# Eight wide and eight narrow products in a row, in place of wide and narrow in turn, in the first half of two MLPs

## The chip, the cores and the metric

The kernel runs on one core of a Trainium2 chip. The metric is the device time of one execution in microseconds. A core has five engines with queues of their own: TensorE (PE in the profile, with its weight loads listed apart as PEld), VectorE (DVE), ScalarE (ACT), GpSimd (POOL) and SyncE (SP), which here issues the DMA transfers.

## The reference, cut to what matters

A trunk of two layers on 256 tokens of width 1024. Layer 0 mixes tokens with differential attention, layer 1 with a sparse attention that picks keys by an indexer; each is followed by an MLP with a squared ReLU. All is float32.

```python
def sq_relu_mlp(h, w1, w2):          # h: 256 x 1024, w1: 1024 x 4096, w2: 4096 x 1024
    u = jax.nn.relu(h @ w1)
    return (u * u) @ w2

for i in range(DEPTH):               # 2
    h = rms_norm(x, norm_mix[i])
    mix = diff_attention(h, ...) if i % 2 == 0 else dsa_attention(h, ...)
    x = x + mix
    x = x + sq_relu_mlp(rms_norm(x, norm_mlp[i]), mlp_w1[i], mlp_w2[i])
```

## The kernel before, in words

TensorE multiplies in a shortened float32 format. To keep the precision, each operand is split in two: a high part (the value rounded to that format) and a low part (what the rounding left). A product A x B is then made of three: high x high, high x low and low x high. The weights arrive by DMA in units of 128 x 2048 (`raw`); `unit` splits each into `whi` (a copy on ACT, L146) and `wlo` (a subtraction on DVE, L147), in two to four pieces. There are four buffers of `whi` and four of `wlo`. The activations are split likewise into the two halves of a tile `act`: `hi`, `lo`, and `both`, a view of the two side by side.

An MLP goes through FF = 4096 in eight blocks of 512 columns. `up(b)` computes block b of h @ w1 transposed: the weights are the stationary operand and the 256 tokens the moving one. A block has four groups m of 128 columns, a group has eight steps k of 128 rows. In each step the high weights meet `both` in one wide product of 512 columns (L479; the left half of the PSUM tile `ps` collects high x high, the right half high x low), and the low weights meet `hi` in one narrow product of 256 columns, added into the right half (L480). `post` then adds the two halves, squares, and splits the result (L485 to L489). The second half of the MLP uses `mm3` (L151, L153, L155): three products of 512 columns each, with the activations stationary. The order is up(0), then for each b: up(b+1), second half of block b. In up(0) the steps are cut in two (k = 0 to 3 for all four groups, then 4 to 7), since the second half of h is finished late; two of its four tiles are `acc`, all others `wk` (four buffers each).

Outside the MLPs, generators (`spawn`, `tick`) lay the attention's small work between the products of `mm3`; `tick` is called in `mm3` alone. The instructions of an engine run in the order in which the framework laid them at compile time; it goes by the written order, but can put an instruction ahead of another where it reckons that operands are late, as it does with the transposes of `make_h` (L228) at the start of an MLP.

Of the kernel before, what the change touches and what calls it, by code (L numbers as in the profile page):

```python
# [45 lines left out]
def trunk(ctx: ExitStack, tc: tile.TileContext, x_in, pos_in, pack_in, wf, out):  # L46
# [11 lines left out]
    mm = nc.tensor.matmul  # L58

    def acc():  # L60
        return psum.tile([128, 512], F32, name="acc", bufs=4)

    def wk():
        return psum.tile([128, 512], F32, name="wk", bufs=4)
# [66 lines left out]
    def unit(cols=2048, dmas=1, pieces=1, between=None):  # L131
        raw = wraw.tile([128, 2048], F32, name="raw")
        hi = wsp.tile([128, 2048], F32R, name="whi")
        lo = wsp.tile([128, 2048], F32R, name="wlo")
        src = bass.AP(tensor=wf.tensor, offset=wf.offset + off[0], ap=[[cols, 128], [1, cols]])
        off[0] += 128 * cols
        step = cols // dmas
        for i in range(dmas):
            c = slice(i * step, (i + 1) * step)
            nc.sync.dma_start(raw[:, c], src[:, c])  # L140
            if between is not None and i == 0:
                between()
        step = cols // pieces
        for i in range(pieces):
            c = slice(i * step, (i + 1) * step)
            split[:] = [nc.scalar.activation(hi[:, c], raw[:, c], AF.Copy).ins]  # L146
            nc.vector.tensor_tensor(lo[:, c], raw[:, c], hi[:, c].bitcast(F32), op=OP.subtract)  # L147
        return hi[:, :cols], lo[:, :cols]

    def mm3(ps, ah, al, wh, wl, first, last):  # L150
        mm(ps, ah, wh, start=first, stop=False)  # L151
        tick()
        mm(ps, ah, wl, start=False, stop=False)  # L153
        tick()
        mm(ps, al, wh, start=False, stop=last)  # L155
        tick()
# [37 lines left out]
    def row_scale(need_s):  # L194

        ss = tiny.tile([128, 2], F32, name="rowss")
        for t in range(2):
            j = sc.tile([128, D], F32, name="qn")
            with tc.issue_after(behind[0]):
                nc.scalar.activation(j, x[t], AF.Square, accum_out=ss[:, t:t + 1])  # L200
        v = tiny.tile([128, 2], F32, name="rowv")
        nc.vector.tensor_scalar(v, ss, 1.0 / D, EPS, op0=OP.mult, op1=OP.add)
        s2 = tiny.tile([128, 2], F32, name="rows2")
        nc.vector.reciprocal(s2, v)
        s = None
        if need_s:
            s = const.tile([128, 2], F32, name=f"srow{need_s}")
            nc.vector.tensor_copy(s, rsqrt_start(v, [128, 2]))
        return s, s2

    def parts():

        a = act.tile([128, 2, 4, 256], F32R, name="act")
        return a[:, 0], a[:, 1], a

    def new_h():
        return [parts() for _ in range(2)]
# [244 lines left out]
    def mlp(h, after):  # L462
        NB = FF // 512
        us = {}
        y = None

        def up(b):
            u1 = [unit(pieces=4 if b < 2 else 2) for _ in range(2)]
            uh, ul, _ = parts()
            us[b] = (uh, ul)  # L470
            w = [tuple(a.rearrange("p (k n) -> p k n", n=256) for a in u) for u in u1]

            def group(ps, m, ks):

                wh, wl = w[m // 2]
                c = slice((m % 2) * 128, (m % 2) * 128 + 128)
                for k in ks:
                    hi, _, both = h[k // 4]
                    mm(ps.rearrange("p (a b) -> p a b", b=256), wh[:, k, c], both[:, :, k % 4], start=k == 0, stop=False)  # L479
                    mm(ps[:, 256:], wl[:, k, c], hi[:, k % 4], start=False, stop=k == 7)  # L480

            def post(ps, m):
                r = sc.tile([128, 256], F32, name="sq")
                q = sc.tile([128, 256], F32, name="on")
                nc.scalar.activation(r, ps[:, 256:], AF.Copy)  # L485
                nc.vector.tensor_tensor(r, ps[:, :256], r, op=OP.add)  # L486
                nc.vector.scalar_tensor_tensor(q, r, 0.0, r, op0=OP.max, op1=OP.mult)  # L487
                nc.scalar.activation(uh[:, m], q, AF.Copy)  # L488
                nc.vector.tensor_tensor(ul[:, m], q, uh[:, m].bitcast(F32), op=OP.subtract)  # L489

            if b == 0:
                pss = [(acc() if m < 2 else wk()) for m in range(4)]
                for kk in range(2):
                    for m in range(4):
                        group(pss[m], m, range(kk * 4, kk * 4 + 4))
                for m in range(4):
                    post(pss[m], m)
            else:
                for m in range(4):
                    ps = wk()  # L500
                    group(ps, m, range(8))
                    post(ps, m)

        up(0)
        _, s2 = row_scale(0)
        for b in range(NB):
            if b + 1 < NB:
                up(b + 1)
            if y is None:
                y = [[acc() for _ in range(2)] for _ in range(2)]  # L510
            u2 = [tuple(a.rearrange("p (k n) -> p k n", n=D) for a in unit(pieces=2)) for _ in range(2)]
            uh, ul = us.pop(b)
            last = b + 1 == NB
            order = ([(t, u, n) for t in range(2) for n in range(2) for u in range(2)] if last else
                     [(t, u, n) for u in range(2) for t in range(2) for n in range(2)])
            for t, u, n in order:
                wh, wl = u2[u]
                for i in range(2):
                    k = u * 2 + i
                    c = slice(n * 512, n * 512 + 512)  # L520
                    tc_ = slice(t * 128, t * 128 + 128)
                    mm3(y[t][n], uh[:, k, tc_], ul[:, k, tc_], wh[:, i, c], wl[:, i, c],
                        b == 0 and k == 0, last and k == 3)
                if last and u == 1:
                    for j in range(2):
                        c = slice(n * 512 + j * 256, n * 512 + j * 256 + 256)
                        nc.vector.scalar_tensor_tensor(x[t][:, c], y[t][n][:, j * 256:j * 256 + 256],  # L527
                                                       s2[:, t:t + 1], x[t][:, c], op0=OP.mult, op1=OP.add)
                        after(t, n, j)


    h = new_h()
# [107 lines left out]
    for j in range(4):  # L640
        ps = [acc() for _ in range(2)]
# [11 lines left out]
    h = new_h()  # L653
# [3 lines left out]
    h = h1  # L657
# [10 lines left out]
    cqh, cql, _ = parts()  # L668
# [102 lines left out]
    for n in range(2):  # L771
        ps = [acc() for _ in range(2)]
# [3 lines left out]
    for n in range(2):  # L776
        ps = [acc() for _ in range(2)]
        c = slice(n * 512, n * 512 + 512)
# [51 lines left out]
    h = new_h()  # L830
# [105 lines left out]
```

## Time and profile before

| | |
|---|---|
| median of 3 runs | 609.68 us (608.34 to 611.04) |
| the profiled execution | 610.02 us, span 607.4 us |
| instructions | 8479 |
| PE / DVE / ACT / POOL busy | 593.5 / 428.1 / 368.9 / 19.1 us |
| products at L479 and L480 | 512 each |

The span runs from the first to the last instruction; some 2.6 us of the execution's time lie around it. Busy times are added per engine and overlap between engines. The end of a matmul is modelled, and matmuls overlap on PE: their starts are what the timeline measures. In the timeline the first number is the start, the second the duration, both in us, and neighbours of the same kind are merged (x2), their duration running from the first start to the last end.

### The profile page before, as it was taken

The numbers are of one execution on the slowest core, as the hardware profiler recorded it, in microseconds if no ns is written. First come the engines' busy times: TensorE is split into PE (matmuls) and PEld (weight loads), VectorE is DVE, ScalarE is ACT, GpSimd is POOL, SyncE is SP. The second block draws the span as 40 slices with busy tenths as digits, with TensorE's granted clock in tenths as the row PEclk, the third lists the DMA queues.
The fourth block names the chain that finished last, engine by engine and source line by source line (L and its number), as shares of the span: only waits on it lengthen the run. The fifth ranks groups of instructions, "written<-read, shape, count | busy, mean of one in ns | idle before, by whom it ended". The sixth has DMA issues, their size and how long they took to land.

```text
span 607.4 us, 8479 instructions
## 1 busy us (share of the span) xinstructions
PE 593.5 (98%) x3072; PEld 488.2 (80%) x3072; DVE 428.1 (70%) x1067; ACT 368.9 (61%) x720; POOL 19.1 (3%) x53
## 2 busy tenths in 40 slices
PE   8989999999999999999999899999999999999997
PEld 6767678888888888888787686778888888888886
DVE  5799986579557557656598999766786565666552
ACT  6789987576445444445397589784854454455430
POOL 5600000000000000000000000000000000000000
PEclk9999999999999999999999899999999999999999
DMA  8753453335645564555453226424465555555301
GB/s 311 261 207 145 143 199 132 146 139 209 208 169 183 203 201 161 193 208 169 162 208 140 71 69 209 139 69 140 139 240 185 199 208 177 179 199 206 141 1 70
DMA packets 16025, 102.29 MB, mean 168 GB/s; under 512 B 1904, under 2 KB 2416, under 8 KB 4336
## 3 DMA queue, kind: packets, MB, share of 16 engines
q1 hardware_dynamic: 15696, 101.62, 47.4%
q8 instruction: 24, 0.39, 0.3%
q10 hardware_dynamic: 288, 0.13, 0.1%
q14 instruction: 17, 0.14, 0.1%
HBM read 100.70 MB, written 1.05 MB: 168 GB/s over the span
## 4 chain that ended last, share of the span: by engine, by line
PE 81%; DVE 10%; ACT 3%; POOL 3%; issue 3%; DVEq 0%; POOLq 0%; ACTq 0%
PE wk L479 18%; PE acc L153 15%; PE acc L155 15%; PE acc L151 15%; PE wk L480 9%; DVE wlo L147 4%; DVE s L411 2%; PE wk L429 2%; PE acc L479 1%; PE wk L400 1%; PE wk L228 1%; POOL ang L276 1%; PE wk L384 1%; POOL tp L275 1%; ACT whi L146 1%
## 5 line engine op out<-in xcount | busy, mean ns | idle before, releaser
L147 DVE TENSOR_TENSOR wlo<-raw,whi 128x1024 fp32r<-128x1024 f32 (+2 forms) x210 | 230.0, 1116 | 115.7 <-ACT whi L146 115.5
L146 ACT ACTIVATE whi<-raw 128x1024 fp32r<-128x1024 f32 (+2 forms) x210 | 197.9, 975 | 96.2 <-issue 46.1
L153 PE MATMUL acc<-wlo,act 128*128 128x512 f32 (+1 forms) x504 | 198.8, 394 | 0.6 <-DVE wlo L147 0.6
L151 PE MATMUL acc<-whi,act 128*128 128x512 f32 (+1 forms) x504 | 199.1, 395 | 0.1
L155 PE MATMUL acc<-whi,act 128*128 128x512 f32 (+1 forms) x504 | 198.5, 394 | 0.0
L479 PE MATMUL wk<-act,whi 128*128 128x512 f32 x480 | 169.8, 398 | 0.0
L480 PE MATMUL wk<-act,wlo 128*128 128x256 f32 x480 | 134.7, 281 | 0.0
L155 PEld LDWEIGHTS acc<-whi,act 128*128 128x128 f32 x504 | 95.3, 189 | 19.9 <-issue 1.7
L153 PEld LDWEIGHTS acc<-wlo,act 128*128 128x128 f32 x504 | 95.4, 189 | 19.7 <-DVE wlo L147 1.3
L151 PEld LDWEIGHTS acc<-whi,act 128*128 128x128 f32 x504 | 95.2, 189 | 19.5 <-issue 1.0
L479 PEld LDWEIGHTS wk<-act,whi 128*128 128x128 f32 x480 | 90.1, 188 | 22.0
L480 PEld LDWEIGHTS wk<-act,wlo 128*128 128x128 f32 x480 | 90.7, 189 | 0.5
L488 ACT ACTIVATE act<-on 128x256 fp32r<-128x256 f32 x64 | 26.3, 417 | 57.5 <-DVE on L487 57.5
L422 ACT ACTIVATE s<-s,nb,rs_r 128x128 f32<-128x128 f32 x64 | 34.2, 537 | 6.0 <-DVE nb L420 5.9
L489 DVE TENSOR_TENSOR act<-on,act 128x256 fp32r<-128x256 f32 x64 | 26.8, 424 | 14.5 <-ACT act L488 12.7
L485 ACT ACTIVATE sq<-wk 128x256 f32<-128x256 f32 x60 | 22.4, 375 | 17.6 <-PE wk L480 17.6
L487 DVE SCALAR_TENSOR_TENSOR on<-sq 128x256 f32<-128x256 f32 x64 | 26.6, 421 | 0.9
L486 DVE TENSOR_TENSOR sq<-wk,sq 128x256 f32<-128x256 f32 x60 | 24.9, 418 | 0.0
L232 ACT ACTIVATE act<-wk,pack 128x128 fp32r<-128x128 f32 x64 | 18.5, 377 | 8.1 <-PE wk L228 8.0
L234 DVE SCALAR_TENSOR_TENSOR act<-wk,pack,act 128x128 fp32r<-128x128 f32 x64 | 17.7, 344 | 3.6 <-ACT act L232 3.6
L429 PE MATMUL wk<-pack,s 128*128 128x128 f32 x72 | 15.7, 290 | 2.5 <-DVE s L594 1.7
L527 DVE SCALAR_TENSOR_TENSOR x<-acc,rows,x 128x256 f32<-128x256 f32 x16 | 7.0, 479 | 15.0 <-PE acc L155 15.0
(176 smaller groups left out, 435.6 us busy)
## 6 DMA issues: line engine op xcount, KB each, us to landing
raw<-in_w SPq DMA_DIRECT2D x91, 1024.0 KB, 4.8
x<-in_x SPq DMA_DIRECT2D x4, 256.0 KB, 4.5
raw<-in_w SPq DMA_DIRECT2D x4, 256.0 KB, 5.2
raw<-in_w SPq DMA_DIRECT2D x2, 512.0 KB, 5.8
raw<-in_w SPq DMA_DIRECT2D x1, 984.0 KB, 4.6
raw<-in_w SPq DMA_DIRECT2D x1, 840.0 KB, 4.8
out_dram<-x SPq DMA_DIRECT2D x3, 256.0 KB, 2.0
out_dram<-x SPq DMA_DIRECT2D x2, 128.0 KB, 1.7
```

The costliest lines, as they stand in the source:

```text
L146: split[:] = [nc.scalar.activation(hi[:, c], raw[:, c], AF.Copy).ins]
L147: nc.vector.tensor_tensor(lo[:, c], raw[:, c], hi[:, c].bitcast(F32), op=OP.subtract)
L151: mm(ps, ah, wh, start=first, stop=False)
L153: mm(ps, ah, wl, start=False, stop=False)
L155: mm(ps, al, wh, start=False, stop=last)
L422: nc.scalar.activation(p[:, TS[t]], s[:, TS[t]], AF.Exp, bias=nb[:, t:t + 1], scale=nsc[:, t:t + 1], accum_out=z[t])
L429: nc.tensor.transpose(pt[:, i * 128:(i + 1) * 128], p[:, i * 128:(i + 1) * 128], ident)
L479: mm(ps.rearrange("p (a b) -> p a b", b=256), wh[:, k, c], both[:, :, k % 4], start=k == 0, stop=False)
L480: mm(ps[:, 256:], wl[:, k, c], hi[:, k % 4], start=False, stop=k == 7)
L487: nc.vector.scalar_tensor_tensor(q, r, 0.0, r, op0=OP.max, op1=OP.mult)
L488: nc.scalar.activation(uh[:, m], q, AF.Copy)
L489: nc.vector.tensor_tensor(ul[:, m], q, uh[:, m].bitcast(F32), op=OP.subtract)
```

## The change

In `group`, the loop over the steps k is run twice. The first run issues the wide products of all steps, the second the narrow products. The operands, the PSUM tile and the flags of the first and last product stay as they are.

```diff
                 for k in ks:
-                    hi, _, both = h[k // 4]
-                    mm(ps.rearrange("p (a b) -> p a b", b=256), wh[:, k, c], both[:, :, k % 4], start=k == 0, stop=False)
-                    mm(ps[:, 256:], wl[:, k, c], hi[:, k % 4], start=False, stop=k == 7)
+                    mm(ps.rearrange("p (a b) -> p a b", b=256), wh[:, k, c], h[k // 4][2][:, :, k % 4],
+                       start=k == 0, stop=False)
+                for k in ks:
+                    mm(ps[:, 256:], wl[:, k, c], h[k // 4][0][:, k % 4], start=False, stop=k == 7)
```

## Rows read from the trace of the kernel before

**Rows 1.** The page: busy time of the engines, and the granted clock in 40 slices.
```profile
PE 593.5 (98%) x3072; PEld 488.2 (80%) x3072; DVE 428.1 (70%) x1067; ACT 368.9 (61%) x720; POOL 19.1 (3%) x53
...
PEclk9999999999999999999999899999999999999999
```
**Rows 2.** The page: the chain that ended last, shares by engine.
```profile
PE 81%; DVE 10%; ACT 3%; POOL 3%; issue 3%; DVEq 0%; POOLq 0%; ACTq 0%
```
**Rows 3.** The page's groups of instructions: busy us, mean ns, idle us before.
```profile
L479 PE MATMUL wk<-act,whi 128*128 128x512 f32 x480 | 169.8, 398 | 0.0
L480 PE MATMUL wk<-act,wlo 128*128 128x256 f32 x480 | 134.7, 281 | 0.0
...
L480 PEld LDWEIGHTS wk<-act,wlo 128*128 128x128 f32 x480 | 90.7, 189 | 0.5
```
**Rows 4.** Windows: an up block in each MLP (first, seventh of twelve later ones).
```profile
158.89:170.18 11.29, 11.29 (x65) 9.80 (x64) 7.78 (x13) 6.32 (x10) 0.00 (x0) 1.00 0.51 179
...
459.32:470.61 11.29, 11.29 (x65) 9.80 (x64) 7.78 (x13) 6.32 (x10) 0.00 (x0) 1.00 0.56 189
```
**Rows 5.** Waits of PEld: us in total, times, longest us.
```profile
PEld acc L479 <- DVE act L234: 0.2, 1, 0.2
```
**Rows 6.** Timeline of DVE ahead of the block at 158.89.
```profile
151.00 1.22 DVE L147 TENSOR_TENSOR wlo<-raw,whi 128x1024 fp32r<-128x1024 f32 x1
```
**Rows 7.** Timeline of PE in an up block: three pairs, narrow to narrow.
```profile
160.18 0.28 PE L480 MATMUL wk<-act,wlo 128*128 128x256 f32 x1
160.29 0.40 PE L479 MATMUL wk<-act,whi 128*128 128x512 f32 x1
160.52 0.28 PE L480 MATMUL wk<-act,wlo 128*128 128x256 f32 x1
160.64 0.40 PE L479 MATMUL wk<-act,whi 128*128 128x512 f32 x1
160.88 0.28 PE L480 MATMUL wk<-act,wlo 128*128 128x256 f32 x1
161.00 0.40 PE L479 MATMUL wk<-act,whi 128*128 128x512 f32 x1
161.24 0.28 PE L480 MATMUL wk<-act,wlo 128*128 128x256 f32 x1
```
**Rows 8.** Timeline of PE, start of the MLPs: two wide products eight pairs apart.
```profile
128.56 0.39 PE L479 MATMUL wk<-act,whi 128*128 128x512 f32 x1
...
131.33 0.39 PE L479 MATMUL acc<-act,whi 128*128 128x512 f32 x1
...
434.29 0.40 PE L479 MATMUL wk<-act,whi 128*128 128x512 f32 x1
...
437.12 0.40 PE L479 MATMUL wk<-act,whi 128*128 128x512 f32 x1
```
**Rows 9.** Timeline of PE, amid a second half: eight products apart.
```profile
150.05 0.39 PE L151 MATMUL acc<-whi,act 128*128 128x512 f32 x1
...
151.86 0.39 PE L155 MATMUL acc<-whi,act 128*128 128x512 f32 x1
```
**Rows 10.** Timeline of PE behind an up block's last narrow product.
```profile
170.06 0.28 PE L480 MATMUL wk<-act,wlo 128*128 128x256 f32 x1
170.18 0.40 PE L151 MATMUL acc<-whi,act 128*128 128x512 f32 x1
...
172.05 0.40 PE L155 MATMUL acc<-whi,act 128*128 128x512 f32 x1
```
**Rows 11.** Timeline of PE in block 0 of the first MLP.
```profile
127.28 0.40 PE L480 MATMUL acc<-act,wlo 128*128 128x256 f32 x2
...
127.75 0.28 PE L480 MATMUL acc<-act,wlo 128*128 128x256 f32 x1
```
**Rows 12.** Timeline of PE: products of 328 columns, eight apart.
```profile
311.30 0.31 PE L151 MATMUL acc<-whi,act 128*128 128x328 f32 x1
...
312.50 0.31 PE L155 MATMUL acc<-whi,act 128*128 128x328 f32 x1
```

## The prediction

> **What bounds the kernel now.** I read the page first. TensorE is busy for 593.5 of 607.4 us, no other engine for more than 428.1, and the clock it was granted is at the full level (2.4 GHz) but for one slice [rows 1]. A busy PE is not yet a PE that sets the time, so the chain that ended last comes next: 81% of the span lies on PE in it [rows 2]. The grouped instructions then give the suspects: the wide products at L479 (stationary high weights, 512 columns) and the narrow ones at L480 (stationary low weights, 256 columns), one weight load before each; the loads' recorded length is 188 to 189 ns [rows 3]. The "mean ns" of a matmul is of no use for a sum: it is 398 and 281, yet a pair takes far less, because matmuls overlap. What one costs is the distance from its start to the next start, and that is read from the timeline.
>
> The windows show the stage. A first half of an MLP (L479/L480 for one block of 512 columns of FF, 32 pairs) takes 11.29 us with PE busy throughout [rows 4] (the stretches are cut at the block's first wide product and at the first product of what follows; x65 is the block's 64 and the end of the one before), so 353 ns per pair and 2.82 us for a group of eight pairs. The list of waits has a single entry for these two lines, 0.2 us at the first wide load of an MLP [rows 5]. So the up blocks are purely TensorE's own pace, and whatever the order of products saves or costs there reaches the end of the kernel one for one; nothing on DVE, ACT or the queues has to be argued away.
>
> **The change part by part.** Nothing is added or removed: 512 wide and 512 narrow products, 1024 loads, the same operands and the same PSUM tile. Only their order within a group changes: eight wide, then eight narrow (in the MLP's block 0, four and four, since its k loop is cut in two). The waits move a little. The high weights of k = 4 are now needed four narrow products (some 0.5 us) earlier, the low weights later. The last low weights of the block that starts at 158.89 are being written at 151.00 and take 1.22 us, and they come after the high ones they are the remainder of [rows 6]; with more than 6 us of cover this costs nothing, and without the cover it would cost at most those 0.5 us per half unit. The high weights' buffer is released some 0.9 us earlier, which helps ACT, which is no bound here. The end of a group, and with it the square and the PSUM tile's release, stays where it is.
>
> What is left is the pace of three kinds of neighbours.
>
> *In turn, as now.* Three pairs in a row, from 160.18 to 161.24, take 1.06 us [rows 7]: 353 ns a pair. From wide to narrow it is 0.23, 0.24 and 0.24 (mean 237), from narrow to wide 0.11, 0.12 and 0.12 (mean 117). All twelve later blocks take 11.29 us, so they go at this pace [rows 4]. The two stretches of block 0 and 1 together (64 pairs in each MLP) differ: eight pairs take 2.77 us in the first MLP and 2.83 in the second [rows 8]. The same code can thus run at 346 or 353 ns a pair; which of the two it falls into is fixed at its start and then stays.
>
> *Wide after wide.* In the second half of the MLP, products of 512 columns follow each other: eight starts in 1.81 us, 226 ns each [rows 9]. But not right after narrow ones: from the first wide product behind the block's last narrow one, eight starts take 1.87 us, 234 ns each [rows 10]. The slow pace thus lasts through as many products as a group has. In the new order every run of eight wide products stands behind narrow ones, so 1.87 is the nearer row, and I take it; 1.81 is the other bound.
>
> *Narrow after narrow.* Hardly in the trace. In one place the compiled order puts two narrow products side by side: the two together are recorded at 0.40 us, one alone at 0.28, so the second starts 0.12 after the first [rows 11]. Products of 328 columns follow each other every 150 ns (eight in 1.20 us) [rows 12]; with 226 for 512 columns this lies on a straight line of 0.41 ns a column, and the line gives 120 at 256 columns. From narrow to wide it is 110 to 120 ns, mean 117 [rows 7]. Below, the bound is 110, the shortest distance between the starts of two such products that the rows show. Above, it is the load's full recorded length, 189 [rows 3], if loads cannot follow each other so closely for eight in a row. I take 117, the mean over the transition that the trace shows most often.
>
> The Trainium skill, page "TensorE: Matmul & The Clock Gate", section "LDWEIGHTS (loading the stationary operand)", puts a load at its column count over 1.2 GHz, 107 ns for 128 columns, and the section "Back-to-back issue gap" puts 256 moving columns at about 109. By these a load just fits behind a narrow product, a group would take an estimated 2.60 us in either order, and the change would be worth nothing. The trace's 226 and 150 ns are above that page's 216 and 139, so its level is not this kernel's.
>
> The sum for a group: 1.87 + 8 x 0.117 = 2.80 us, against 2.82 in the twelve later blocks (48 groups) and 2.83 in the second MLP's start (8 groups): about 0.018 less, 56 times, 1.0 us gained. In the first MLP's start (8 groups) 2.77 becomes 2.80: 0.25 us lost. Together 0.75 us less. The profiled execution took 610.02 us, 607.4 of them span, 0.3 above the median of 609.68; so 609.3 for a profiled run and 608.9 as the median. A kernel of this spread (608.34 to 611.04) tells a change from none at about 0.5%, 3.05 us.
>
> **The rivals.**
>
> *The wide runs settle (faster).* If eight narrow products in a row leave less behind than narrow and wide in turn, the wide run goes at 1.81 and the narrow at 0.12: 2.77 a group, the pace the first MLP's start already has. That is 0.05 us in 56 groups, 2.8 us: 606.9. With narrow products at the lower bound of 0.11 too, a group is 2.69: 0.13 x 56 + 0.08 x 8 = 7.9 us, 601.8. For it: the start of the first MLP holds 346 ns per pair for 21 us, so the extra 7 ns are not a fixed price. Against it: after that very row of narrow ones a wide run still goes slowly [rows 10].
>
> *The narrow runs expose their loads (slower).* A wide product gives the next load 226 ns of cover, a narrow one little more than its own 107 ns (256 columns at the line's 0.41); now eight in turn need one load each. At present each load under a narrow product is followed by one under a wide one, which can make up for a late load. If each narrow product pays the 7 ns that a pair pays now, it takes 0.127, the group 2.89, and the kernel 0.07 x 56 + 0.12 x 8 = 4.9 us more: 614.6. At 150, the shortest pace that the trace holds over a long run with a load each, it would be 0.033 x 8 x 64 = 17 us more than the sum above: 626. At 189 the price is 37 us: 646. The point from which it decides (0.5% slower) is 0.124 for narrow after narrow. Against it: the loads of the 328-column run keep to the column line, and the one narrow pair stands at 0.12.
>
> *The order isn't kept.* The pair of narrow products side by side stands in a place where the code alternates [rows 11]: the compiled order is not the written one everywhere. If wide and narrow are laid in turn again, the time stays at 609.7.
>
> **How the numbers follow.** The likeliest case, a small gain by the sum, gets 0.50; its own range is 606.7 to 610.5 (narrow at 0.113 to 0.12, and the spread of the medians). The wide runs settle: 0.27. At 2.77 a group that just misses 0.5% (2.8 of 3.05 us), and any narrow pace under 0.12 passes it, so 0.22 of the 0.27 counts as faster. The narrow runs pay: 0.18, of it 0.17 beyond 0.5%. Order not kept: 0.05. So faster by over 0.5% 0.22, slower 0.17, within it 0.61. The range reaches into both rivals, from 605.6 (half way through the faster one) to 612.6, and leaves out about 0.1 on each side.
>
> **What would show it.** In the timeline of an up block: runs of eight L479 and eight L480; eight wide starts in 1.87 us (1.81 if the faster rival holds); narrow starts 0.117 apart (0.127 and more for the slower one). In the windows: an up block of 11.22 us instead of 11.29; 11.1 or less for the faster rival, 11.5 or more for the slower. Second halves unchanged. No new wait of L479 on the high weights. The prediction is wrong if the granted clock changes in the MLPs, or if stages outside them move by more than 1 us because the instructions there are laid in another order.

## The result, and the profile after

The changed kernel takes 606.59 us in the median of 5 runs (605.23 to 607.85), the one before 609.68 (608.34 to 611.04): ratio 0.9947, 95% interval 0.9923 to 0.9972. In a second series of five rounds, the run `after_again` below, the ratio was 0.9963 (0.9952 to 0.9975). So the change gains 2 to 3 us, 0.3 to 0.5%. The forecast was 608.9 with a range from 605.6 to 612.6: the sign was right and the range held the time, but the gain is some three to four times the 0.75 us of the sum.

The page after shows the same picture as [rows 1, 2]: PE sets the time, with 2.9 us less of it. One thing differs beside that: the one slice in which the granted clock was below its full level is gone.

```profile
PE 590.6 (98%) x3072; PEld 487.5 (81%) x3072; DVE 430.3 (71%) x1067; ACT 367.1 (61%) x720; POOL 19.0 (3%) x53
...
PEclk9999999999999999999999999999999999999999
...
PE 79%; DVE 13%; POOL 3%; issue 3%; ACT 3%; DVEq 0%; POOLq 0%; ACTq 0%
```

The windows of the changed kernel, cut as in [rows 4] (an up block, the second half behind it, the last up block): a later up block takes 11.15 us (11.146 by the start times in the trace) in place of 11.29, and the second half behind it 10.90 or 10.91, where the trace of before has 10.94. A row of a window has the stretch, its length, the busy time of PE, PEld, DVE, ACT and POOL with their instructions, the granted clock (1.00 is the full level), the share of DMA and its GB/s. First the second half of before, then the changed kernel:

```profile
170.18:181.12 10.94, 10.94 (x50) 9.02 (x49) 6.13 (x8) 4.71 (x6) 0.00 (x0) 1.00 0.51 191
```

```profile
159.33:170.48 11.15, 11.15 (x66) 9.83 (x65) 8.19 (x13) 6.91 (x11) 0.00 (x0) 1.00 0.64 220
170.48:181.38 10.90, 10.90 (x50) 9.01 (x49) 5.91 (x7) 4.00 (x6) 0.00 (x0) 1.00 0.46 159
...
567.67:578.81 11.14, 11.14 (x65) 9.82 (x64) 8.19 (x13) 6.91 (x11) 0.00 (x0) 1.00 0.20 83
```

The timeline of that first block answers to [rows 7] and [rows 10] at once, since runs of one kind are merged into a row. L478 is now the wide product, L481 the narrow one.

```profile
159.33 1.98 PE L478 MATMUL wk<-act,whi 128*128 128x512 f32 x8
161.14 1.11 PE L481 MATMUL wk<-act,wlo 128*128 128x256 f32 x8
162.09 2.00 PE L478 MATMUL wk<-act,whi 128*128 128x512 f32 x8
163.94 1.12 PE L481 MATMUL wk<-act,wlo 128*128 128x256 f32 x8
164.89 2.00 PE L478 MATMUL wk<-act,whi 128*128 128x512 f32 x8
166.73 1.12 PE L481 MATMUL wk<-act,wlo 128*128 128x256 f32 x8
167.68 2.00 PE L478 MATMUL wk<-act,whi 128*128 128x512 f32 x8
169.52 1.11 PE L481 MATMUL wk<-act,wlo 128*128 128x256 f32 x8
170.47 0.40 PE L151 MATMUL acc<-whi,act 128*128 128x512 f32 x1
```

Read by starts: the block's first wide run takes 1.81 us (159.33 to 161.14), because it stands behind wide products of the second half; the three others, behind narrow runs, take 1.85, 1.84 and 1.84. Every narrow run takes 0.95, so 119 ns a product. By the single starts in the trace a wide run behind a narrow one goes 234, 235, 229, 232, 231, 227, 226, 227 ns: the slow pace lasts five products, not eight, and costs 27 ns in all. A narrow run goes 113, then 119 and 120.

**Where the 3.0 us between the two profiled spans (607.4 and 604.4) lie**, by start times in the two traces: the twelve later up blocks 12 x 0.144 = 1.73; the second halves behind them 12 x 0.036 = 0.43; the stretch from the second MLP's first wide product to its third up block 0.18 (34.58 to 34.40); the missing dip of the clock between the MLPs (a fall to its lower level, 1.2 GHz) 1.1; against this 0.19 lost in the first MLP's start (34.17 to 34.36) and 0.25 ahead of it. Without the dip the products' pace and the rest are worth 1.9 us, ratio 0.997, which lies in both intervals.

### The profile page after: what moved, and what is told of

Same layout as the page of the kernel before. It is cut to its first block, busy times and chain, and to the rows that moved or that the text cites. A ratio compares the mean times of both kernels' runs of the same rounds, so it can differ in the third digit from the quotient of the medians.

```text
span 604.4 us, 8481 instructions
## 1 busy us (share of the span) xinstructions
PE 590.6 (98%) x3072; PEld 487.5 (81%) x3072; DVE 430.3 (71%) x1067; ACT 367.1 (61%) x720; POOL 19.0 (3%) x53
## 4 chain that ended last, share of the span: by engine, by line
PE 79%; DVE 13%; POOL 3%; issue 3%; ACT 3%; DVEq 0%; POOLq 0%; ACTq 0%
PE wk L478 18%; PE acc L153 14%; PE acc L155 14%; PE acc L151 14%; PE wk L481 9%; DVE wlo L147 4%; DVE s L411 2%; PE wk L429 2%; PE acc L478 1%; PE wk L400 1%; PE wk L228 1%; DVE score L759 1%; DVE qkss L367 1%; DVE m L758 1%; POOL ang L276 1%
## 5 line engine op out<-in xcount | busy, mean ns | idle before, releaser
L146 ACT ACTIVATE whi<-raw 128x1024 fp32r<-128x1024 f32 (+2 forms) x210 | 195.7, 973 | 89.9 <-issue 46.2
L478 PE MATMUL wk<-act,whi 128*128 128x512 f32 x480 | 120.6, 392 | 0.0
L478 PEld LDWEIGHTS wk<-act,whi 128*128 128x128 f32 x480 | 86.8, 189 | 15.8
L481 PEld LDWEIGHTS wk<-act,wlo 128*128 128x128 f32 x480 | 66.0, 190 | 5.1
L481 PE MATMUL wk<-act,wlo 128*128 128x256 f32 x480 | 67.5, 282 | 0.0
```

Of the source, the lines that this page charges most:

```text
L478: mm(ps.rearrange("p (a b) -> p a b", b=256), wh[:, k, c], h[k // 4][2][:, :, k % 4], start=k == 0, stop=False)
L481: mm(ps[:, 256:], wl[:, k, c], h[k // 4][0][:, k % 4], start=False, stop=k == 7)
```

## The experiments

**The unchanged and the changed kernel once more** (no edit in either).

> The unchanged kernel, profiled a second time. In the first profile the granted clock fell to its lower level once between the MLPs, at 356 us, and in the changed kernel's profile it did not. If that dip belongs to the order of the work, it is there again at the same place, and the stretch between the MLPs is again about 1.1 us longer than in the changed kernel. If it is chance, it is gone or elsewhere, and the span falls from 607.4 to about 606.3. Either way the up blocks take 11.29 us and the start of each MLP falls into one of its two paces, 347 or 354 ns a pair.

> The changed kernel again, in five rounds. If the gain is all in the pace of the products (0.14 us in each of the twelve later up blocks, 0.036 in the second half behind each, some 0.3 in the second MLP's start), it is 2.0 to 2.5 us, ratio 0.996 to 0.997. If the missing clock dip belongs to the change, it is 3.0 us again, ratio 0.995.

Before: 610.89 us (one run), span 608.3. After: 607.80 (606.66 to 608.09), ratio 0.9963 as above. The up blocks repeat to the last digit: 11.290 and 11.146 us. The dip is back in the kernel before, behind the same place (345 us in the first profile, not the 356 of the expectation; 347 in this one): PE waits 2.2 us for L355, and the clock falls to its lower level within 0.6 us after the wait ends. The changed kernel has the wait too, and no dip. The windows of 7 us behind the end of that wait, kernel before and then changed kernel, with the granted clock in the third column from the right:

```profile
346.50:353.50 7.00, 7.00 (x28) 5.74 (x29) 7.00 (x24) 4.87 (x9) 0.00 (x0) 0.76 0.01 2
```

```profile
345.67:352.67 7.00, 7.00 (x35) 5.71 (x36) 7.00 (x24) 6.08 (x12) 0.00 (x0) 1.00 0.01 2
```

At 0.76 PE runs 28 products in that time, at 1.00 it runs 35. In the twelve profiles of this study the wait of 2.1 to 2.2 us is in each, and the dip behind it in three: both of before and `apart` (whose blocks take as long as before's); not in `widths_turn`, which has wide and narrow in turn as well. Another dip, at 36 to 37 us, stands in seven of them, of before and after alike. So wide and narrow in turn alone doesn't make it. But the three that have it are all three whose blocks take 11.29 us, and none of the nine others has it: that it belongs to the timing of the kernel before is not ruled out, and it is left out of the price of the products below, not shown to be chance. The mean clock of each execution on record says how many dips it had, though not where: none (0.999 or 1.0) in 9 of 29 of the kernel before and in 11 of 33 of the changed kernel and its longer runs; two (0.994 or less) in 3 and in none. In the second series all six executions of the changed kernel have one dip (0.996 or 0.997), so its gain doesn't come from fewer of them; this series, the less favourable one, is also the one nearer to the sum of the blocks (2.0 us against 1.9).

The start of the second MLP of before took 34.22 us this time, not 34.58: it fell into the quicker of its two paces. So the same code differs in this from one execution to the next.

**Longer runs.** The up blocks from 1 on are issued over two or over all four groups. (The edits here and below are cut to what matters; `wide` and `narrow` issue the one product of group m and step k.)

```diff
-                for m in range(4):
-                    ps = wk()
-                    group(ps, m, range(8))
-                    post(ps, m)
+                for g in range(0, 4, 2):             # runs32: range(0, 4, 4), four tiles
+                    ps = {m: wk() for m in range(g, g + 2)}
+                    for m in ps:
+                        for k in range(8):
+                            wide(ps[m], m, k)
+                    for m in ps:
+                        for k in range(8):
+                            narrow(ps[m], m, k)
+                        post(ps[m], m)
```

> Sixteen wide products of two groups, then their sixteen narrow ones. Theory of the switch: a change from narrow to wide costs about 27 ns in all, spread over the next five wide products, a change from wide to narrow gives 7 back, and all else goes at 227 (wide) and 120 ns (narrow). Then a later up block goes from 11.146 to 11.107 us, and the kernel is 0.5 us faster than with runs of eight: about 606.1 against 606.6. Theory of the single product (each narrow product in a run is cheap by itself, the wide one after it pays whatever the run's length): no difference to runs of eight.

> All 32 wide products of an up block, then its 32 narrow ones. Theory of the switch: no wide run of an up block stands behind narrow products any more, a block takes 11.086 us, and the kernel is 0.7 us faster than with runs of eight, about 605.9. The four PSUM tiles are all in use at once, so if the squares at the end of a block come late, the second half or the next block waits for them, and that would eat the gain: the rival says 606.6 or more, with a wait of PE on ACT or DVE at the up blocks' end.

Measured: 607.01 us (604.36 to 607.38), ratio 0.9939 (0.9920 to 0.9957), and 606.73 (605.42 to 606.86), ratio 0.9942 (0.9930 to 0.9954). The blocks take 11.106 and 11.086 us, as the cost of a switch has it (11.107 and 11.086), and not the 11.146 of the theory of the single product. An up block and the second half behind it in each, by windows, first runs16, then runs32:

```profile
160.26:171.37 11.11, 11.11 (x66) 9.84 (x65) 6.73 (x10) 6.98 (x10) 0.00 (x0) 1.00 0.50 190
171.37:182.27 10.90, 10.90 (x51) 9.02 (x49) 6.73 (x10) 3.64 (x7) 0.00 (x0) 1.00 0.51 195
```

```profile
160.23:171.31 11.08, 11.08 (x65) 9.83 (x64) 4.01 (x5) 6.57 (x8) 0.00 (x0) 1.00 0.53 193
171.31:182.22 10.91, 10.91 (x50) 9.03 (x49) 9.26 (x16) 4.03 (x8) 0.00 (x0) 1.00 0.50 183
```

With runs of 32 the squares move into the second half (DVE's busy time is 4.01 us in the block and 9.26 in the second half, 8.19 and 5.91 with runs of eight), and no wait of PE on ACT or DVE stands in the later up blocks or at their ends. The rival of the late squares falls. Both kernels are faster than the one before beyond their intervals; against runs of eight the trace decides (0.04 and 0.06 us a block), since the intervals of the whole kernel overlap.

**The length of the runs, by block.** One kernel, another length in each block; `equal` below adds more.

```diff
+                n = (0, 1, 2, 4, 8, 16, 32, 8)[b]
+                seq = [(m, k) for m in range(4) for k in range(8)]
+                for i in range(0, 32, n):
+                    # n wide products of seq[i:i + n], then their n narrow ones
```

> The length of the runs differs by block: in each MLP block 1 has wide and narrow in turn, block 2 runs of two, block 3 of four, 4 of eight, 5 of sixteen, 6 of 32, 7 of eight. Theory of the switch (wide 227, narrow 120, each switch from narrow to wide 27 ns over five products, each switch to narrow 7 back): blocks of 11.29, about 11.23, 11.19 to 11.25, 11.146, 11.107, 11.086 us, then 11.146. Rival (what counts is whether a narrow product stands behind another): runs of two already have most of the gain, 11.15 or less.

Measured: 607.63 us against 610.25 for the kernel before on the same chip (one run each). Us per block, the same in both MLPs to 0.001: 11.136 at 2, 11.200 at 4, 11.146 at 8, 11.106 at 16, 11.086 at 32; in turn (from before) 11.290. From 4 up the cost of a switch holds. At 2 it doesn't (11.23 expected): the rival's number comes out (11.15 or less), but not its reason, for two at a time is better than four or eight. The windows of blocks 2 and 3 and the timeline of block 2:

```profile
160.44:171.57 11.13, 11.13 (x65) 9.72 (x64) 7.82 (x13) 6.31 (x10) 0.00 (x0) 1.00 0.52 193
182.46:193.66 11.20, 11.20 (x65) 9.80 (x64) 8.09 (x13) 6.53 (x11) 0.00 (x0) 1.00 0.56 195
```

```profile
161.12 0.63 PE L475 MATMUL wk<-act,whi 128*128 128x512 f32 x2
161.59 0.39 PE L480 MATMUL wk<-act,wlo 128*128 128x256 f32 x2
161.82 0.63 PE L475 MATMUL wk<-act,whi 128*128 128x512 f32 x2
162.28 0.40 PE L480 MATMUL wk<-act,wlo 128*128 128x256 f32 x2
162.51 0.63 PE L475 MATMUL wk<-act,whi 128*128 128x512 f32 x2
```

Two wide take 0.46 or 0.47, so they are slow (233, 236 and 233, 231 ns); but the two narrow take 0.23 (116 and 112, 113 and 119), well under 0.24. In turn and in runs of four the narrow products give back less than the wide ones lose.

**What makes the wide product slow.** Three causes were tried. First the width of the narrow product, in turn and in runs of eight:

```diff
+                v = (256, 256, 224, 192, 128, 288, 320, 384)[b]
+                i, j = min((k % 4) * 256, 1024 - v), 256 if v <= 256 else 512 - v
-                mm(ps[:, 256:], w[m // 2][1][:, k, c], h[k // 4][0][:, k % 4], start=False, stop=k == 7)
+                mm(ps[:, j:j + v], w[m // 2][1][:, k, c], flat[:, i:i + v], start=False, stop=k == 7)
```

> Wide and narrow in turn as before, but the narrow product has another number of columns in each block: 256, 224, 192, 128, 288, 320, 384 in blocks 1 to 7 (fewer: part of the product low x high is left out; more: columns of the neighbouring k are added that the reference doesn't have). The straight line of the column pace gives 347, 333, 320, 293, 360, 373, 400 ns a pair. Theory of the late load (a load needs about 110 ns, a 256-column product covers it by too little): 288 columns and more keep to the line, 256 is 6 to 7 ns above it, and from 224 down the pair stays near 340 whatever the width. Rival of the mixed shapes (any change of width costs): about 7 ns above the line everywhere, at 320 and 384 too.

> The same widths in runs of eight. Theory of the late load: at 288, 320 and 384 columns the first wide products behind a narrow run go at 227 at once, with no slow ones; at 224, 192 and 128 narrow products stay at 108 to 113 ns each whatever the width, and the slow tail is as long as at 256 or longer. Rival of the mixed shapes: the tail of 234, 235, 229, 232, 231 stands behind narrow runs of every width, and narrow products go down along the line (107, 93, 67 ns).

Measured: 612.75 us in turn and 611.66 in runs, against 610.25 for the kernel before (one run each; the work isn't the same). The windows of blocks 2 to 7 (224, 192, 128, 288, 320, 384 columns), in turn, and behind them in runs:

```profile
159.97:170.95 10.98, 10.98 (x65) 9.58 (x64) 7.32 (x11) 5.78 (x9) 0.00 (x0) 1.00 0.52 193
181.85:192.70 10.85, 10.85 (x65) 9.53 (x64) 7.24 (x11) 5.78 (x9) 0.00 (x0) 1.00 0.54 193
203.62:214.45 10.83, 10.83 (x66) 9.52 (x64) 7.56 (x12) 5.89 (x9) 0.00 (x0) 1.00 0.51 189
225.41:237.08 11.67, 11.67 (x66) 10.27 (x65) 8.00 (x13) 6.32 (x10) 0.00 (x0) 1.00 0.50 181
248.00:260.14 12.14, 12.14 (x66) 10.79 (x65) 8.12 (x13) 6.31 (x10) 0.00 (x0) 1.00 0.51 178
271.04:284.04 13.00, 13.00 (x65) 11.60 (x64) 8.19 (x13) 6.31 (x10) 0.00 (x0) 1.00 0.52 186
```

```profile
159.23:170.13 10.90, 10.90 (x66) 9.58 (x64) 7.84 (x12) 5.74 (x10) 0.00 (x0) 1.00 0.60 205
181.04:191.88 10.84, 10.84 (x65) 9.55 (x64) 7.84 (x12) 5.73 (x10) 0.00 (x0) 1.00 0.56 203
202.80:213.70 10.90, 10.90 (x65) 9.52 (x64) 7.84 (x12) 5.80 (x10) 0.00 (x0) 1.00 0.55 201
224.68:236.17 11.49, 11.49 (x65) 10.23 (x64) 8.28 (x13) 6.91 (x11) 0.00 (x0) 1.00 0.58 225
247.06:259.06 12.00, 12.00 (x66) 10.68 (x64) 8.09 (x13) 7.05 (x11) 0.00 (x0) 1.00 0.58 212
269.96:282.99 13.03, 13.03 (x66) 11.66 (x64) 8.28 (x13) 7.29 (x12) 0.00 (x0) 1.00 0.56 213
```

In turn, per pair: 343, 339 and 338 ns at 224, 192 and 128 columns (the line has 333, 320, 293), 365, 379 and 406 at 288, 320 and 384 (the line has 360, 373, 400). Below 256 the pair stops falling: it costs some 112 to 116 ns more than a wide product, however few columns the narrow one has. In runs, too, the narrow products are 107 to 117 ns apart (but the first of a run, which goes at 100, 85 and 58, while the wide product behind the run takes 237, 253 and 292). That half of the late-load theory holds. The other half falls: at 320 and 384 columns the narrow product takes 147 and 175 ns, far more than the floor of 112, and the pair still pays 6 ns over the line. In runs the picture is uneven: behind 288 columns the wide run goes at 227 at once (11.49 us a block, under the line's 11.52), behind 320 and 384 the slow products are back, and at 384 and at 128 runs of eight are no better than in turn (13.03 against 13.00, 10.90 against 10.83). The rival of the mixed shapes expected a tail behind every width, which 288 denies, and narrow products falling along the line below 256, which they don't.

Second, the columns of PSUM. The narrow products got a tile of their own:

```diff
+                    ps, ps2 = wk(), wk()
-                mm(ps[:, 256:], w[m // 2][1][:, k, c], h[k // 4][0][:, k % 4], start=False, stop=k == 7)
+                mm(ps2[:, :256], w[m // 2][1][:, k, c], h[k // 4][0][:, k % 4], start=k == 0, stop=k == 7)
...
                 nc.vector.tensor_tensor(r, ps[:, :256], r, op=OP.add)
+                nc.vector.tensor_tensor(r, ps2[:, :256], r, op=OP.add)
```

> Wide and narrow in turn as before, but from block 1 on the narrow products collect in a PSUM tile of their own, added by one more DVE operation per group; so a narrow product no longer adds to the columns that the wide product before it has just written. Theory of the late load: no difference, 353 ns a pair, 11.29 us a block. Rival (the narrow product waits for the wide one's sums in the same columns): 347 ns a pair, 11.09 us a block. With two tiles a group of the four, PE may also wait for a free tile; that would show as idle time before a group's first product.

Measured: 610.34 us against 610.25 for the kernel before on the same chip (one run each). All twelve later blocks take 11.290 us, with the same distances between starts as in [rows 7]. Adding into columns just written costs nothing here; that cause falls.

```profile
159.46:170.75 11.29, 11.29 (x66) 9.80 (x64) 8.88 (x15) 5.78 (x9) 0.00 (x0) 1.00 0.54 187
```

Third, lengths against operands:

```diff
+                            if b == 1:               # the low weights meet both halves
+                                wide(ps, m, k)
+                                mm(ps.rearrange("p (a b) -> p a b", b=256), wl, both, start=False, stop=k == 7)
+                            else:                    # b == 2: the wide product in two
+                                for i in range(2):
+                                    mm(ps[:, i * 256:i * 256 + 256], wh, both[:, i], start=k == 0 and i == 0, stop=False)
+                                narrow(ps, m, k)
```

> Again another pattern in each block. Block 1: in turn, but the narrow product is made as wide as the other (512 columns: the low weights meet the low activations too, which only adds a smaller term to the sum). Block 2: in turn, but the wide product is cut into two of 256 with the same weights, so that all are narrow. Theory of unequal lengths: equal neighbours keep to the line, 453 ns a step and 14.51 us for block 1, 360 ns a step and 11.52 us for block 2, and in block 2's case no product of 512 columns is there to be slow. Rival (it is the change between high and low weights, or between two-piece and one-piece moving operands, that costs): block 1 pays the 7 ns per step as well, 14.72 us. Blocks 3 to 7: runs of 3, 5, 6, 12 and 24, to see whether the cost falls steadily with the length (it did from 4 on: 11.200, 11.146, 11.106, 11.086 us at 4, 8, 16, 32) or whether the 11.136 at 2 is one of several exceptions: by a fixed cost per switch 11.22, 11.18, 11.16, 11.12 and 11.11.

Measured: 615.95 us (one run), with the longer products in it. The windows of block 1 (512 and 512 in turn) and block 2 (all 256), and block 1's timeline amid it:

```profile
137.78:152.34 14.56, 14.56 (x67) 12.02 (x65) 11.83 (x22) 7.37 (x14) 0.00 (x0) 1.00 0.59 199
163.22:174.73 11.51, 11.51 (x97) 11.51 (x96) 7.90 (x13) 6.31 (x10) 0.00 (x0) 1.00 0.51 183
```

```profile
140.10 0.39 PE L475 MATMUL wk<-act,whi 128*128 128x512 f32 x1
140.32 0.39 PE L514 MATMUL wk<-act,wlo 128*128 128x512 f32 x1
140.55 0.39 PE L475 MATMUL wk<-act,whi 128*128 128x512 f32 x1
140.78 0.39 PE L514 MATMUL wk<-act,wlo 128*128 128x512 f32 x1
```

High and low weights in turn, the same PSUM tile, and yet every product costs 227 ns (the 0.05 us over 14.51 lie in the first nine products, behind block 0's narrow ones), and all-narrow goes at 120 ns through 96 products. So the change between high and low weights doesn't cost. The other half of the rival is not in this run: in block 1 both moving operands are of two pieces, in block 2 all are of one. The trace of the changed kernel settles it. In the second half every moving operand is of one piece. From its products to the block's first wide ones the number of pieces changes and the length doesn't, and those go at 227 at once (1.81 us for eight, above). From the narrow run to the second half the length changes and the pieces don't, and there the slow pace of 234, 235, 229, 232, 231 ns stands again, 1.84 us for eight:

```profile
170.47 0.40 PE L151 MATMUL acc<-whi,act 128*128 128x512 f32 x1
...
172.31 0.39 PE L155 MATMUL acc<-whi,act 128*128 128x512 f32 x1
```

So it is at a change of length that the cost appears, and the operands don't make it. The run lengths 3, 5, 6, 12 and 24 gave 11.185, 11.190, 11.170, 11.126 and 11.106 us: from 5 up within 0.01 of the fixed cost per switch (11.18, 11.16, 11.12, 11.11); 3 is better than that rule, as 2 was.

**Block 0 in long runs too.** The same edit in the loop over the two halves of k, on top of runs32.

> All 32 wide products of a block, then its 32 narrow ones, and block 0 in runs of sixteen and sixteen in each half of its k loop, in place of four and four. By the cost of a switch block 0 loses six of its eight switches in each MLP, some 0.1 us each time: 0.2 us under the version before it, so 0.994 of the unchanged kernel's time; more than a measurement of the whole kernel can tell apart, so the start of the MLPs in the trace decides (from the first wide product to the second block's second half).

Measured: 606.48 us (605.61 to 607.21), ratio 0.9958 (0.9942 to 0.9974). The starts of the MLPs, the deciding stretch, take 34.33 and 34.40 us against runs32's 34.31 and 34.36: nothing gained. The timeline behind block 0 shows where it went: the compiled order breaks block 1's run. By the single starts block 1 takes 11.21 us so, and 11.13 in runs32; one distance of 308 ns, behind the first wide product after the four narrow ones, is the most of it, and block 0's gain of 0.06 us is gone. Why the order is broken is not shown. Block 1 needs four `wk` tiles, two of which were block 0's just before; but that is so in runs32 too, where block 1's 32 wide products stand together.

```profile
136.72 3.82 PE L475 MATMUL wk<-act,whi 128*128 128x512 f32 x16
140.38 0.63 PE L480 MATMUL wk<-act,wlo 128*128 128x256 f32 x4
140.87 3.88 PE L475 MATMUL wk<-act,whi 128*128 128x512 f32 x16
144.58 3.52 PE L480 MATMUL wk<-act,wlo 128*128 128x256 f32 x28
```

## Why the prediction was right, and which terms were off

*Sign and size.* The sign came out for the reason given, but the size did not, and it is the width of the range, which reaches into the rivals on both sides, that held the time, so that is in part luck: the median of 606.59 lies just below the likeliest case's own range (606.7 to 610.5) and beside the faster rival's 606.9. By the trace a later block gains 0.144 us where the sum had 0.07; 11.146 lies between the 11.22 of the forecast and the 11.1 of that rival.

*The stage is PE's own pace.* Right. Nothing but PE's order changed the blocks, and no wait of PE on ACT or DVE appeared in the later up blocks. The earlier need of high weights cost nothing there.

*In turn costs 353 ns a pair, the start of an MLP 347 or 353.* Right wherever that order ran. But the pace isn't fixed at the start for good: in `apart` the first MLP's start went at 347 until the compiled order put four wide and four narrow products together, and at 353 behind them.

*Wide after narrow: 1.87 us for eight.* Mis-sized in two ways. Behind a narrow run eight take 1.84, because the slow pace lasts five products: the row taken for it stood behind wide and narrow in turn, where it lasts ten. And it was applied to all four groups of a block, though the first one stands behind a second half and goes at 1.81. Together that is 3 x 0.03 + 0.06 = 0.15 us a block.

*Narrow after narrow: 0.117.* It is 0.119, within the bounds; 32 x 0.002 = 0.06 us a block the other way. Together that is some 0.08 us: the block came out at 11.146 where the forecast had 11.22, 12 times, some 0.9 us in all.

*Second halves unchanged.* Wrong. [rows 10] showed that their first products pay for what stands ahead of them; behind a narrow run they pay less than behind wide and narrow in turn. 12 x 0.036 = 0.43 us, left out of the sum although the row was in hand.

*The first MLP's start loses 0.25 us.* Right: 0.19 in the first profiles. The second MLP's start gained 0.18 against the first profile of before and lost as much against the second: that goes by the pace that the kernel before fell into.

*The rivals.* That wide runs settle came half true: they settle after five products. That narrow runs expose their loads did not happen at 256 columns (120 ns stays under the 0.124 that would decide) but is near: the floor of some 112 ns, seen below 256, leaves 8 ns. (The 107 ns of that rival should read 105, 256 times 0.41; no sum uses it.) The written order was kept in the later blocks.

*The rest of the difference between the first two profiles*, some 1.1 us, is the clock's dip between the MLPs, which the forecast had named only as a thing that would make it wrong within the MLPs.

What stays open is why TensorE runs a product more slowly behind a shorter one. Shown is that equal lengths never paid it; that the operands and the PSUM columns don't make it, nor, at 320 and 384 columns, a load that comes late; that the cost is spread over several products; and that it depends unevenly on widths and run lengths (none behind a run of 288 columns, little at runs of two). Unequal lengths don't always pay it either: the quicker pace at the start of an MLP, 347 ns a pair (230 and 117), is just the sum of the steady 227 and 120. A block in turn at that pace would take an estimated 11.09 us (32 x 0.3467), as little as with runs of 32. What puts all twelve later blocks of the kernel before into the slower pace is open too.

## What to carry to other kernels

Where TensorE is busy throughout, add up start-to-start distances, not durations, and take them behind the neighbour that the new order gives; then look at what stands behind the edited stage as well, for it may pay for its end. Products of one length in long runs went at a steady pace here, 227 and 120 ns; a run of narrow products between wide ones cost some 20 ns net (27 behind it, 7 given back in it), and the fewest changes, one per block, were the best of those tried. That is no rule for short runs: runs of two beat runs of four here. A gain of 0.5% needs a second series and a look at the clock's row before it is believed: here a third of the difference between the first two profiles was the clock.

## What had not been expected of the hardware

Eight products of 512 columns behind a run of 256 take 234, 235, 229, 232, 231, 227, 226, 227 ns: a cost spread over five products that are alike. The same alternating order can settle at 347 or at 353 ns a pair and keep either for some 20 us. In runs at 224 columns or fewer a product with its load costs 107 to 117 ns, but for the first. The Trainium skill, page "TensorE: Matmul & The Clock Gate", section "LDWEIGHTS (loading the stationary operand)", gives 107 ns for a load of 128 columns; this floor agrees with it nearly.
